# A two-layer attention and state-space backbone on one core: half of the chunk input matrices made one stage earlier, one state copy on another engine

## The chip, the core and the metric

The kernel runs on one core of a Trainium2 chip. Its time is the device time of one execution in microseconds (us); lower is better. The engines are TensorE (PE in the profile; PEld is its weight load), VectorE (DVE), ScalarE (ACT), GpSimd (POOL) and SyncE (SP), which here only issues DMAs.

## What is computed

The reference is a backbone of two layers over 2048 latent tokens and 256 context tokens of width 1024, all in float32. Layer 0 is windowed attention with sinks; layer 1 is a bidirectional diagonal state-space layer (S5), and only layer 1 is touched here. Cut to that:

```python
u, z = split(h @ w_in, 2);  uc = hc @ w_in[:, :1024]     # 64 groups of 16 channels
for dirn in range(2):
    a_bar = exp(lam * dt);  b_bar = ((a_bar - 1) / lam)[..., None] * b_mat     # complex, 64 states per group
    bu = einsum('gph,blgh->blgp', b_bar, u)              # 'bu_c' the same for the context
    xs = diag_scan(a_bar, bu with the context's end state added)               # second direction on flipped rows
    y += einsum('ghp,blgp->blgh', c_mat, xs).real
out = ((glu(gelu(y) @ w_glu)) * silu(z)) @ w_out
```

The kernel cuts the 2304 tokens into 144 chunks of 16. What one chunk adds to the 64 complex states of a group is a product of the chunk's 16 x 16 inputs with a matrix E[t, h] = a_bar^(15 - t) * b_bar[h], a power of a_bar times a column of b_bar: these are the chunk input matrices, 2 (real, imaginary) x 64 groups of [128 x 256], where the 128 partitions are 2 directions x 64 states.

## The kernel before

Layer 1 goes through these stages.

**u projection** (`phase3`, lines 1236 to 1306). For u = 0 to 7, each a pair of row tiles, `prep(u + 1)` loads rows of x by DMA (SP queue, L1255), norms them, transposes them on TensorE, and splits them into a high and a low part (`split`, L106 to L111); `mm(u, j, n)` then multiplies with weights already in SBUF, three matmuls per product (L116 to L118), and ScalarE copies the result into `uy` (L1287). Beside it, `ssm_bc` (from L384) makes the tables of c and b and stores them in the DRAM tensor `tabd`; it is a generator that is stepped once per u for u = 1 to 5. `tabd[sl]` holds, for 8 groups, the powers (rows 0, 1) and b_bar (rows 2, 3).

**Chunk states** (`phase4`, lines 1309 to 1399). For sl = 0 to 7 (8 groups each) it loads `tab` from `tabd` (L1340) and the context's u (L1342), and copies the latter into place on VectorE (`uc`, L1350). For each half `hf` (4 groups) it makes the real and imaginary chunk matrices `er`, `ei`: two products and a sum each, with one product of each pair on GpSimd (`em`, L1365 and L1368), the other and the sum on VectorE (L1366, L1367, L1369, L1370). `er` and `ei` have two buffers each, one per half. For each group TensorE transposes E (four transposes into `ep`, L1382; ScalarE copies them to `esb`, L1384), transposes u (`up`, L1389 and L1390; three of four are copied back by VectorE, L1394, one by ScalarE, L1392), and one group behind multiplies both into `st` (L1329, `chunk_states`; two PSUM buffers). Three ScalarE copies take `st` to `sall`: the forward states (L1331), and the backward states in reversed order in two parts (L1332, L1333). In `sall` the group is the innermost index, so that a copy writes single floats at a stride.

**Scan and z projection** (`scan` from L1405, `zproj` from L1427). The scan over the 143 chunks is a chain of products and sums on VectorE alone (L1420, L1425). Meanwhile TensorE does the z projection (tiles `zps`), whose weights and rows are loaded over SP (L1445, L1457, tile `zraw`) and split. Its SBUF tiles lie over those of the stage before: a load starts when the tile below it has had its last reader. The first product of the scan is pinned, by `keep`, behind the VectorE instructions written before it, which are the splits of the first weights and of the first two row pieces.

**Outputs** (`phase5`, `phase6`, `phase7`) follow; none of their lines is edited.

The source is not the order of issue: a planner simulates the program and gives each engine's queue its order, which is then fixed. Each queue runs in order, and an instruction that waits holds up all behind it.

Of the kernel before, what the change touches and what calls it, by code (L numbers as in the profile page):

```python
# [6 lines left out]
F32 = mybir.dt.float32  # L7
# [3 lines left out]
AF = mybir.ActivationFunctionType  # L11
OP = mybir.AluOpType
# [60 lines left out]
P3O = 'P0 C01 C11 P1 M00 M10 M01 M11'  # L73
LO = 'x21 yt0 ogh1 gate1 zt0 zt1 vt1 x20 ogh2 ogh3 ogl2 ogl3 ogh0 ogl0 ogl1 gate0 vt0'
LO4 = 'tab4_0 tab4_1 em_0 uc4_1 uc4_0 esb_0 esb_1 esb_2 esb_3 ucr4_0 er_0 ei_0 em_1 er_1 ei_1'
UCA = 'vvvvvvvv'
HP = 0
ZC = 5
# [7 lines left out]
class Net:  # L86
# [1149 lines left out]
    def phase3(self, uy):  # L1236
        nc, a = self.nc, self.a
        with ExitStack() as es:
            es.callback(self.kpool.__exit__, None, None, None)
            es.callback(self.esm3.close)  # L1240
            es.callback(self.es3.close)
            ex, wq, sq = self.ex3, self.wu, self.sq3
            x0 = self.xp3.tile([128, 2, D], F32, name="xt3")
            for j in range(2):
                nc.sync.dma_start(x0[:, j], self.xrows(j))
            xh = ex.enter_context(self.pool("p3xh", 1, side="right"))
            sm = es.enter_context(self.pool("p3s", 2))
            ps = es.enter_context(self.pool("p3ps", 2, PSUM))
            H = {-1: self.hc}

            def prep(u):
                if u:
                    xs = self.kp.tile([128, 2, D], F32, name=("qta", "qtb")[u % 2])
                    for j in range(2):
                        nc.sync.dma_start(xs[:, j], self.xrows(2 * u + j))  # L1255
                else:
                    xs = x0
                ss = sq.tile([128, 2], F32, name="ss3")
                for j in range(2):
                    junk = sq.tile([128, D], BF16, name="junk3", bufs=1)  # L1260
                    nc.scalar.activation(junk, xs[:, j], AF.Square, accum_out=ss[:, j:j + 1])
                r = self.rstd(sq, ss, 2)
                for j in range(2):
                    (nc.vector if u == 0 and j == 0 else nc.gpsimd).tensor_scalar(xs[:, j], xs[:, j], r[:, j:j + 1], 1.0, op0=OP.mult,
                                                                                  op1=OP.mult)
                hi = sm.tile([128, KT, 256], F32R, name="hi3")
                lo = sm.tile([128, KT, 256], F32R, name="lo3")
                for k in range(0, KT, 2):
                    self.prep3(k, lambda j, c: xs[:, j, c:c + 128], ps.tile([128, 2, 256], F32, name="tp3"), hi, lo, 0,
                               self.h1d[u][:, k:k + 2],  # L1270
                               xh.tile([128, 2, 256], F32, name=f"hf{k}") if u == 0 and k < 4 else None)
                H[u] = (hi, lo)

            def mm(u, j, n):
                hi, lo = H[u]
                c = slice(j * 128, (j + 1) * 128)
                p = self.mmp.tile([128, 512], F32, name="mm3")
                for q in range(2):
                    w = wq[n * 2 + q]
                    self.mm3(p[:, q * 256:(q + 1) * 256], lambda k: hi[:, k, c], lambda k: lo[:, k, c],  # L1280
                             lambda k: w[0][:, k], lambda k: w[1][:, k], KT)
                if u < 0:
                    self.ctx_out(j, n, p)
                    return
                for q in range(4):
                    o = uy[n * 4 + q][:, :, (15 - 2 * u - j) * 16:(16 - 2 * u - j) * 16]
                    nc.scalar.activation(o, p[:, q * 128:(q + 1) * 128].rearrange("p (g h) -> p g h", h=16), AF.Copy)  # L1287

            for tok in P3O.split():
                if tok[0] == "P":  # L1290
                    prep(int(tok[1]))
                else:
                    mm(0 if tok[0] == "M" else -1, int(tok[1]), int(tok[2]))
            for u in range(1, 8):
                if u + 1 < 8:
                    prep(u + 1)
                for j in range(2):
                    for n in range(2):
                        mm(u, j, n)
                if u == 1:  # L1300
                    ex.close()
                    bp = es.enter_context(self.pool("p3b", 1, side="right"))
                    bps = es.enter_context(self.pool("p3bps", 1, PSUM))
                    bc = self.ssm_bc(bp, bps)
                if 1 <= u <= 5:
                    next(bc)


    def phase4(self, uy, sall):
        nc, a = self.nc, self.a  # L1310
        with ExitStack() as es:
            pool4 = es.enter_context(self.pool("p4", 1))
            size4 = {"tab4": 512, "ucr4": 2048, "uc4": 2048, "esb": 512}
            for nm in LO4.split():
                pool4.tile([128, size4.get(nm.split("_")[0], 1024)], F32, name=nm)
            turn = {}

            def T4(name, shape, n):
                i = turn[name] = turn.get(name, -1) + 1
                return pool4.tile(shape, F32, name=f"{name}_{i % n}")  # L1320

            ps = es.enter_context(self.pool("p4ps", 2, PSUM))
            pend = []

            def chunk_states(esb, u, g):
                st = ps.tile([128, 2, 144], F32, name="st", bufs=PB[2])
                for ri in range(2):
                    for b in range(2):
                        nc.tensor.matmul(st[:, ri], esb[:, ri, b], u[:, b * 144:(b + 1) * 144], start=b == 0, stop=b == 1)  # L1329
                sv = sall.rearrange("p j r g -> p r j g")  # L1330
                nc.scalar.activation(sv[0:64, :, :, g], st[0:64], AF.Copy)  # L1331
                nc.scalar.activation(self.rev(sall, 64, 128, 15, 16, g), st[64:128, :, 0:16], AF.Copy)  # L1332
                nc.scalar.activation(self.rev(sall, 64, 128, 143, 128, g), st[64:128, :, 16:144], AF.Copy)  # L1333

            for sl in range(8):
                hp4 = ExitStack()
                if sl < HP:
                    hp4.enter_context(self.tc.manual_schedule(engines={nc.vector.engine}))
                tab = T4("tab4", [128, 4, 8, 16], 2)
                nc.sync.dma_start(tab, self.tabd[sl, :, 0:4].rearrange("p j (g h) -> p j g h", g=8))  # L1340
                ucr = T4("ucr4", [16, 16, 128], 1)
                nc.sync.dma_start(ucr, self.ucd[:, sl * 128:(sl + 1) * 128].rearrange("(c t) n -> c t n", t=16))  # L1342
                uc = T4("uc4", [16, 8, 256], 2)
# [2 lines left out]
                cv = ucr.rearrange("c t (g h) -> c t g h", h=16)  # L1346
                if UCA[sl] == "a":
                    nc.scalar.activation(uv, cv, AF.Copy)
                else:
                    (nc.vector if UCA[sl] == "v" else nc.gpsimd).tensor_copy(uv, cv)  # L1350
                E = []
                for hf in range(2):
                    gs = slice(hf * 4, hf * 4 + 4)

                    def pw(j):
                        return tab[:, j, gs, :, None].to_broadcast([128, 4, 16, 16])

                    def bb(j):
                        return tab[:, 2 + j, gs, None, :].to_broadcast([128, 4, 16, 16])

                    er = T4("er", [128, 4, 16, 16], 2)
                    ei = T4("ei", [128, 4, 16, 16], 2)
                    m = T4("em", [128, 4, 16, 16], 2)
                    m2 = T4("em", [128, 4, 16, 16], 2)
                    nc.gpsimd.tensor_tensor(m, pw(1), bb(1), op=OP.mult)  # L1365
                    nc.vector.tensor_mul(er, pw(0), bb(0))  # L1366
                    nc.vector.tensor_sub(er, er, m)  # L1367
                    nc.gpsimd.tensor_tensor(m2, pw(1), bb(0), op=OP.mult)  # L1368
                    nc.vector.tensor_mul(ei, pw(0), bb(1))  # L1369
                    nc.vector.tensor_add(ei, ei, m2)  # L1370
                    E.append((er, ei))
                hp4.close()
                for hf in range(2):
                    er, ei = E[hf]
                    for gg in range(4):
                        g = sl * 8 + hf * 4 + gg
                        gl = hf * 4 + gg
                        ep = ps.tile([128, 2, 2, 128], F32, name="ep", bufs=PB[0])
# [7 lines left out]
                        u = uy[sl][:, gl]  # L1386
# [543 lines left out]
    def run(self, dbg=None):  # L1930
        nc, tc, a = self.nc, self.tc, self.a
        with ExitStack() as es:
            dr = es.enter_context(tc.tile_pool(name="dram", bufs=1, space=DRAM))
# [2 lines left out]
            self.vd = dr.tile([NTILE, 128, 4, 128], F32, name="vd")  # L1936
            self.zd = dr.tile([NTILE, 128, 8, 128], F32, name="zd")
            self.x1d = dr.tile([NTILE, 128, D], F32, name="x1d")
            self.modd = [dr.tile([2, 3 * D], F32, name=f"mod{i}") for i in range(2)]
            self.tabd = dr.tile([8, 128, 9, 128], F32, name="tabd")  # L1940
            self.a16d = dr.tile([128, 2, 64], F32, name="a16d")
# [16 lines left out]
            with self.pool("sall", side="right") as sp:  # L1958
                sall = sp.tile([128, 144, 2, 64], F32, name="sall")
# [63 lines left out]
```

## Time and profile before

| | us |
|---|---|
| median of 3 runs (2672.64 to 2676.73) | 2673.79 |
| the profiled execution | 2675.37 |
| its span, first to last instruction | 2673.5 |
| TensorE busy | 2540.4 (95%) |
| VectorE busy | 1624.3 (61%) |
| ScalarE busy | 1190.1 (45%) |
| GpSimd busy | 933.2 (35%) |

Busy shares are averages over unlike stages, and a TensorE matmul's recorded time includes its pipeline, so that back-to-back matmuls overlap in the record. The stages have to be read one by one. All starts below are us from the start of the span.

### The profile page before, as it was taken

Reading aid. Unit: us, or ns where it says so; the run is one execution under the profiler, and the core shown is the slowest. Engines: PE = TensorE matmul, PEld = TensorE weight load, DVE = VectorE, ACT = ScalarE, POOL = GpSimd, SP = SyncE. Lnnn points to the kernel's source line nnn. Section 1 sums busy time; section 2 is a strip of 40 time slices with the busy share of each in tenths; the row PEclk is TensorE's granted clock in tenths of the full one; section 3 lists DMA queues with packets and bytes.
Section 4 is the critical chain, followed back from the end, with each engine's and each line's share of the span. In section 5 each row is a group of like instructions: output and inputs, shape, how many; then the busy total and the mean of one; then the engine's idle time right before and its main releaser. Section 6 shows DMA issues by size and latency. Waiting matters only on the chain. (4 is left out here: it accounts for less than half of the span.)

```text
span 2673.5 us, 43894 instructions
## 1 busy us (share of the span) xinstructions
PE 2540.4 (95%) x15973; PEld 2273.4 (85%) x15973; DVE 1624.3 (61%) x3816; ACT 1190.1 (45%) x2711; POOL 933.2 (35%) x778
## 2 busy tenths in 40 slices
PE   7999999998999999999899999899489899999998
PEld 5999989987988999998899988899467688888887
DVE  4772377537888888888531288799976431002454
ACT  3201210137777777777443178633189820001221
POOL 0321331213554455555241163355255222221221
PEclk9999999999999999999999989999789999999999
DMA  8464446477453434343363100344133332223542
GB/s 285 166 180 140 141 153 191 140 206 183 109 127 96 105 99 118 84 109 106 110 168 99 32 25 13 118 143 156 49 91 94 94 86 63 81 61 122 170 143 85
DMA packets 374330, 317.22 MB, mean 119 GB/s; under 512 B 64210, under 2 KB 327394, under 8 KB 374114
## 3 DMA queue, kind: packets, MB, share of 16 engines
q1 hardware_dynamic: 264722, 235.64, 31.8%
q10 hardware_dynamic: 109392, 78.76, 9.2%
q8 instruction: 127, 2.08, 0.3%
q14 instruction: 89, 0.73, 0.1%
HBM read 225.63 MB, written 88.70 MB: 118 GB/s over the span
## 5 line engine op out<-in xcount | busy, mean ns | idle before, releaser
L116 PE MATMUL mm<-hhl,whi 128*128 128x384 f32 x848 | 286.9, 341 | 3.6 <-DVE whi L108 2.7
L934 POOL TENSOR_SCALAR P<-P,ri 128x640 f32<-128x640 f32 (+2 forms) x272 | 208.7, 780 | 228.4 <-DVE ri L932 187.4
L117 PE MATMUL mm<-hhl,whi 128*128 128x384 f32 x848 | 286.8, 338 | 0.0
L118 PE MATMUL mm<-hhl,wlo 128*128 128x384 f32 x848 | 285.2, 337 | 0.6 <-DVE wlo L111 0.6
L953 DVE TENSOR_TENSOR pl<-pt,ph 128x512 fp32r<-128x512 f32 (+1 forms) x384 | 233.2, 607 | 32.6 <-ACT ph L952 30.0
L912 DVE CUSTOM_DVE_ANT_0 P<-S,mask,sink 128x640 f32<-128x640 f32 (+1 forms) x240 | 209.2, 872 | 55.9 <-PE S L903 50.6
L952 ACT ACTIVATE ph<-pt 128x512 fp32r<-128x512 f32 (+1 forms) x384 | 202.9, 529 | 73.2 <-PE pt L948 70.5
L948 PE MATMUL pt<-ident,P 128*128 128x128 f32 x1312 | 212.6, 274 | 13.0 <-DVE pl L953 5.2
L913 ACT ACTIVATE P<-P,nm 128x640 f32<-128x640 f32 (+1 forms) x256 | 208.1, 813 | 23.7 <-DVE nm L912 7.7
L948 PEld LDWEIGHTS pt<-ident,P 128*128 128x128 f32 x1312 | 156.6, 140 | 31.3 <-POOL P L934 10.8
L111 POOL TENSOR_TENSOR wlo<-wraw,whi 128x512 fp32r<-128x512 f32 x60 | 86.6, 1472 | 259.0 <-DVE whi L108 252.7
L116 PEld LDWEIGHTS mm<-hhl,whi 128*128 128x128 f32 x848 | 159.5, 189 | 14.3 <-issue 9.9
L117 PEld LDWEIGHTS mm<-hhl,whi 128*128 128x128 f32 x848 | 160.2, 189 | 6.5 <-issue 6.1
L118 PEld LDWEIGHTS mm<-hhl,wlo 128*128 128x128 f32 x848 | 160.0, 189 | 1.3 <-DVE wlo L111 0.9
L116 PE MATMUL zps<-zh,wzh 128*128 128x256 f32 x512 | 146.0, 287 | 5.1 <-ACT zo L1496 4.3
L117 PE MATMUL zps<-zh,wzh 128*128 128x256 f32 x512 | 146.2, 287 | 2.4 <-POOL zh L111 2.4
L1852 DVE TENSOR_TENSOR gy<-gps,gs 128x512 f32<-128x512 f32 x32 | 22.1, 691 | 207.4 <-POOL gs L1850 207.4
L118 PE MATMUL zps<-zh,wzl 128*128 128x256 f32 x512 | 145.9, 286 | 0.0
L1425 DVE TENSOR_TENSOR sall<-sall 128x64 f32<-128x64 f32 x560 | 141.6, 309 | 0.1
L1849 ACT ACTIVATE gs<-gps 128x512 f32<-128x512 f32 x32 | 19.1, 597 | 258.6 <-PE gps L118 258.6
L108 DVE CAST whi<-wraw 128x512 fp32r<-128x512 f32 (+1 forms) x80 | 53.5, 719 | 106.7 <-PE mm L117 86.7
L111 POOL TENSOR_TENSOR zh<-zraw,zh 128x512 fp32r<-128x512 f32 x61 | 81.6, 1344 | 101.6 <-ACT zh L106 78.3
(591 smaller groups left out, 7735.3 us busy)
## 6 DMA issues: line engine op xcount, KB each, us to landing
qta<-qd SPq DMA_DIRECT2D x144, 128.0 KB
qtb<-qd SPq DMA_DIRECT2D x144, 128.0 KB
wraw<-in_w_ada_dram SPq DMA_DIRECT2D x16, 1024.0 KB
zraw<-h1d SPq DMA_DIRECT2D x64, 256.0 KB
wraw<-in_attn_w_in_dram SPq DMA_DIRECT2D x12, 1024.0 KB
mq<-qqd SPq DMA_DIRECT2D x64, 192.0 KB
qd<-oh ACTq DMA_DIRECT2D x48, 192.0 KB
qd<-ol ACTq DMA_DIRECT2D x48, 192.0 KB
```

The lines of the kernel that those rows point to most:

```text
L108: nc.vector.tensor_copy(hi, src)
L111: (nc.gpsimd if lo_eng == "g" else nc.vector).tensor_tensor(lo, src, hi.bitcast(F32), op=OP.subtract)
L116: nc.tensor.matmul(ps, whi(k), mhi(k), start=first and k == 0, stop=False)
L117: nc.tensor.matmul(ps, whi(k), mlo(k), start=False, stop=False)
L118: nc.tensor.matmul(ps, wlo(k), mhi(k), start=False, stop=last and k == nk - 1)
L912: nc.vector.tensor_tensor_reduce(o, sc, mk, -0.125, nsink[:, h:h + 1], OP.add, OP.min, nm)
L913: nc.scalar.activation(p, p, AF.Exp, bias=nm, scale=-1.0, accum_out=SM[i][:, e:e + 1])
L934: (nc.vector if e >= CTXV else nc.gpsimd).tensor_scalar(P[i][e], P[i][e], ri[:, e:e + 1], 1.0, op0=OP.mult, op1=OP.mult)
L948: ins = nc.tensor.transpose(t[:, c - c0], P[i][e][:, k * 128:(k + 1) * 128], self.ident)
L952: nc.scalar.activation(ph[:, c0:c1], t, AF.Copy)
L953: nc.vector.tensor_tensor(pl[:, c0:c1], t, ph[:, c0:c1].bitcast(F32), op=OP.subtract)
L1425: nc.vector.tensor_add(y[:, :, hs[h]], t[:, h, i], y[:, :, hs[h]])
```

## The change

Three edits. (1) For sl = 0, 2, 4, 6 the chunk matrices are made in the u projection by a new generator, `chunk_in`: 16 pieces of 2 groups, at u = 3 to 6, each with six VectorE instructions (one product goes to PSUM, none to GpSimd) and two DMAs of 256 KB to a new DRAM tensor `ed`; `phase4` then loads `er` and `ei` from `ed` in four DMAs of 512 KB per sl, and leaves out `tab` and the making for these. (2) The steps of `ssm_bc` come earlier: two at u = 1, two at u = 2, one at u = 3; then its SBUF pool is closed and a pool for the pieces opened. (3) The larger part of the backward states' copy (L1333) goes from ScalarE to VectorE.

```diff
+PRE = (0, 2, 4, 6)
...
-                if 1 <= u <= 5:
+                for _ in range((0, 2, 2, 1, 0, 0, 0, 0)[u]):
                     next(bc)
+                if u == 3:
+                    eb.close()
+                    ep = es.enter_context(self.pool("p3e", 2, side="right"))
+                    eg = self.chunk_in(ep, bps)
+                if u >= 3:
+                    for _ in range(4):
+                        next(eg, None)
+            for _ in eg:
+                pass
+
+    def chunk_in(self, pool, ps):
+        nc = self.nc
+        for sl in PRE:
+            tab = pool.tile([128, 4, 8, 16], F32, name="tab3", bufs=1)
+            nc.sync.dma_start(tab, self.tabd[sl, :, 0:4].rearrange("p j (g h) -> p j g h", g=8))
+            for hq in range(4):
+                gs = slice(hq * 2, hq * 2 + 2)
...
+                for ri, op in enumerate((OP.subtract, OP.add)):
+                    e = pool.tile([128, 2, 16, 16], F32, name="e3" + "ri"[ri])
+                    m = ps.tile([128, 512], F32, name="ctp2", bufs=1).rearrange("p (g t h) -> p g t h", g=2, t=16)
+                    nc.vector.tensor_mul(e, pw(0), bb(ri))
+                    nc.vector.tensor_mul(m, pw(1), bb(1 - ri))
+                    nc.vector.tensor_tensor(e, e, m, op=op)
+                    nc.sync.dma_start(self.ed[sl, ri, :, hq * 512:(hq + 1) * 512], e.rearrange("p g t h -> p (g t h)"))
+                yield
...
-                nc.scalar.activation(self.rev(sall, 64, 128, 143, 128, g), st[64:128, :, 16:144], AF.Copy)
+                nc.vector.tensor_copy(self.rev(sall, 64, 128, 143, 128, g), st[64:128, :, 16:144])
...
-                tab = T4("tab4", [128, 4, 8, 16], 2)
-                nc.sync.dma_start(tab, self.tabd[sl, :, 0:4].rearrange("p j (g h) -> p j g h", g=8))
+                if sl not in PRE:
+                    tab = T4("tab4", [128, 4, 8, 16], 2)
+                    nc.sync.dma_start(tab, self.tabd[sl, :, 0:4].rearrange("p j (g h) -> p j g h", g=8))
...
+                    if sl in PRE:
+                        for ri, e in enumerate((er, ei)):
+                            nc.sync.dma_start(e.rearrange("p g t h -> p (g t h)"),
+                                              self.ed[sl, ri, :, hf * 1024:(hf + 1) * 1024])
+                        E.append((er, ei))
+                        continue
```

## Rows read from the trace of the kernel before

**Rows 1.** Busy time by stretch: start:end, length, engine busy (instructions), clock, DMA share, GB/s.
```profile
1420.00:1530.00 110.00, 110.00 (x940) 110.00 (x940) 13.99 (x33) 30.94 (x109) 17.09 (x12) 1.00 0.18 59
1530.60:1697.90 167.30, 159.24 (x1041) 133.95 (x1040) 134.06 (x131) 128.47 (x276) 73.80 (x32) 0.94 0.10 28
1697.90:1928.40 230.50, 191.62 (x1550) 188.06 (x1548) 228.92 (x878) 72.52 (x159) 100.91 (x80) 0.92 0.41 125
```

**Rows 2.** Timeline of TensorE after the z projection: start, us, instruction, idle before.
```profile
1929.76 3.78 PE L1669 MATMUL yp<-uy,xT 128*128 128x256 f32 x8 [32.68 <-ACT xT L1664]
```

**Rows 3.** Timeline of TensorE, two matmul groups of the steady part of `phase4`.
```profile
1653.00 1.25 PE L1329 MATMUL st<-uy,esb 128*128 128x144 f32 x8
...
1655.31 1.25 PE L1329 MATMUL st<-uy,esb 128*128 128x144 f32 x8
```

**Rows 4.** Timelines where `phase4` begins: a wait of TensorE, then one of VectorE.
```profile
1534.39 0.23 PE L1390 MATMUL up<-ident,uc 16*128 16x16 f32 x1 [3.31 <-DVE uc L1350]
...
1527.96 1.23 DVE L1369 TENSOR_TENSOR ei<-tab 128x1024 f32<-128x1024 f32 x1 [14.65 <-PE mm L118]
```

**Rows 5.** Timeline of TensorE around a stall in the middle of `phase4`.
```profile
1594.55 0.33 PE L1389 MATMUL up<-ident,uy 128*128 128x128 f32 x1 [0.77 <-DVE uy L1394]
...
1595.39 1.52 PE L1329 MATMUL st<-uy,esb 128*128 128x144 f32 x8
...
1602.86 1.32 PE L1329 MATMUL st<-uy,esb 128*128 128x144 f32 x8
```

**Rows 6.** Waits of TensorE in `phase4`: us in total, times, longest.
```profile
PE st L1329 <- ACT sall L1333: 3.4, 11, 0.6
```

**Rows 7.** Timelines where `phase4` hands over: TensorE, SP queue, VectorE, TensorE.
```profile
1687.53 0.38 PE L1382 MATMUL ep<-ident,ei 128*128 128x128 f32 x2
...
1688.37 5.67 SPq L1457 DMA_DIRECT2D zraw<-h1d  x4
...
1695.48 1.38 DVE L1420 TENSOR_TENSOR kps<-sall,bco 128x128 f32<-128x128 f32 x1
...
1696.12 0.38 PE L116 MATMUL zps<-zh,wzh 128*128 128x256 f32 x1
```

**Rows 8.** Groups of VectorE in `phase4`: busy us, mean ns, idle before and releaser.
```profile
L1370 DVE TENSOR_TENSOR ei<-ei,em 128x1024 f32<-128x1024 f32 x16 | 33.2, 2077 | 1.5 <-POOL em L1368 1.5
L1366 DVE TENSOR_TENSOR er<-tab 128x1024 f32<-128x1024 f32 x15 | 24.1, 1608 | 9.5 <-PE ep L1382 9.5
L1369 DVE TENSOR_TENSOR ei<-tab 128x1024 f32<-128x1024 f32 x15 | 23.4, 1560 | 0.0
L1367 DVE TENSOR_TENSOR er<-er,em 128x1024 f32<-128x1024 f32 x16 | 21.1, 1317 | 1.5 <-POOL em L1365 1.5
L1394 DVE COPY uy<-up 128x288 f32<-128x288 f32 x48 | 21.0, 446 | 7.3 <-PE up L1390 7.2
L1350 DVE COPY uc<-ucr 16x2048 f32<-16x2048 f32 x8 | 13.3, 1665 | 0.4 <-DMA ucr<-ucd 0.4
```

**Rows 9.** Group of ScalarE in `phase4`: the copy that moves.
```profile
L1333 ACT ACTIVATE sall<-st 64x256 f32<-64x256 f32 x64 | 38.5, 602 | 0.0
```

**Rows 10.** One VectorE line before: a copy read at a stride, duration ns min/median/max.
```profile
L365 DVE COPY pwg<-pr x1: 1082/1082/1082, 537.9 to 537.9; 64x1024 f32<-64x1024 f32 x1
```

**Rows 11.** VectorE lines of 512 elements: sum in SBUF; product into PSUM (ns min/median/max).
```profile
L425 DVE TENSOR_TENSOR bx<-bx,by x4: 676/690/1604, 1353.5 to 1378.7; 128x512 f32<-128x512 f32 x4
...
L1536 DVE TENSOR_TENSOR ytp<-tab x4: 685/894/1111, 1928.4 to 1933.2; 128x512 f32<-128x512 f32 x4
```

**Rows 12.** Timelines: two loads of 512 KB issued, and the reader of the second.
```profile
1439.68 0.81 SPq L1255 DMA_DIRECT2D qtb<-x1d  x2
...
1446.16 1.06 ACT L1261 ACTIVATE junk<-qtb 128x1024 bf16<-128x1024 f32 x1 [1.19 <-DMA qtb<-x1d]
```

**Rows 13.** Timelines: last split of `prep(7)` on GpSimd, first matmul of u = 7.
```profile
1490.98 1.29 POOL L111 TENSOR_TENSOR lo<-kctx,hi 128x512 fp32r<-128x512 f32 x1 [2.40 <-DVE hi L108]
...
1507.90 0.28 PE L116 MATMUL mm<-kall,hi 128*128 128x256 f32 x1
```

More of the change, by code (lines that the diff above doesn't have):

```diff
@@ L1301, in phase3, with pw, bb @@
                     ex.close()
-                    bp = es.enter_context(self.pool("p3b", 1, side="right"))
+                    eb = ExitStack()
+                    bp = eb.enter_context(self.pool("p3b", 1, side="right"))
                     bps = es.enter_context(self.pool("p3bps", 1, PSUM))
                     bc = self.ssm_bc(bp, bps)
-                if 1 <= u <= 5:
+                for _ in range((0, 2, 2, 1, 0, 0, 0, 0)[u]):
                     next(bc)
+                if u == 3:
[14 more added lines that the diff above has]
+                gs = slice(hq * 2, hq * 2 + 2)
+                def pw(j):
+                    return tab[:, j, gs, :, None].to_broadcast([128, 2, 16, 16])
+                def bb(j):
+                    return tab[:, 2 + j, gs, None, :].to_broadcast([128, 2, 16, 16])
+                for ri, op in enumerate((OP.subtract, OP.add)):
[6 more added lines that the diff above has]
+                yield
     def phase4(self, uy, sall):
@@ L1938, in run @@
             self.x1d = dr.tile([NTILE, 128, D], F32, name="x1d")
+            self.ed = dr.tile([8, 2, 128, 2048], F32, name="ed")
             self.modd = [dr.tile([2, 3 * D], F32, name=f"mod{i}") for i in range(2)]
```

## The prediction

> **What bounds the kernel now.** I first read the busy times of three stretches around the edits [rows 1]. In the u projection (1420 to 1530) TensorE is busy in all 110 us, at the full clock; VectorE has 14.0 of 110. In `phase4` (1530.6 to 1697.9) the granted clock is 0.94 and VectorE has 134 of 167. In the scan (1697.9 to 1928.4) VectorE has 228.9 of 230.5: it alone sets the end, and TensorE, done early, stands idle for 32.7 us before the outputs [rows 2]. So the u projection can take VectorE work, and what counts at the other side is not when the z projection starts but when the scan starts.
>
> What does `phase4` cost at best? In its steady part TensorE goes from one group's `st` to the next in 2.31 us (1655.31 - 1653.00) [rows 3]; 64 groups make 147.8. The stage took 165.5, from its first transposes at 1530.6, where I set the edge of the stretch [rows 1], to the first `zps` matmul at 1696.1 [rows 7]. The 17.7 between them lie in three places. At the start TensorE waits 3.31 us for VectorE's `uc`, which stood behind chunk products [rows 4]. [...] At the end it waits 3.4 us for `st` buffers that ScalarE has not copied [rows 6]. The remainder, 10.7, I put down to the start: the 3.31 and the slow clock behind it, with about 2 of scatter.
>
> How does this stage hand over? The scan's first product is pinned behind splits of rows whose loads need the tiles of E. The last transposes of E end at 1687.9 (1687.53 + 0.38); the loads go out at 1688.4, and the scan starts at 1695.5, 7.6 after the last transposes [rows 7]. The last `st` ends only at 1696, since transposes ran ahead of the ScalarE-bound `st`.
>
> **The change, part by part.**
> *Making in `phase4`.* The four making lines hold 101.8 us of VectorE [rows 8]; half of it goes, 51, and half of their partner products on GpSimd.
>
> *The moved copy.* ScalarE loses 64 x 0.602 = 38.5 us [rows 9], from 128 to 90 of 167: the 3.4 at the end goes. VectorE gains 64 copies. No row shows one that writes single floats at a stride. From the PSUM copy of 288 columns, 446 ns [rows 8], 256 columns cost at least 0.40 each, 25.6 in all; as on ScalarE, 0.60, they would be 38.5. [...] With the copies of `up` (21.0) and `uc` (13.3) VectorE then has 51 + 25.6 + 34.3 = 111 us in some 155, or 124 at the dear end.
>
> But it is uneven. A half's E can be made only while the other half is consumed, 4 x 2.31 = 9.2 us, and takes 101.8 / 16 = 6.4 on average. With three copies of `up` (1.3), four new copies (1.6) and half a `uc` (0.8) that window needs 10.1 of 9.2, twice in a row for each of sl = 1, 3, 5, 7; in the windows of the loaded halves it needs 3.7. TensorE can fill by transposing u ahead, as it does now. I count one stall as now, 3.6, between none and the eight windows' 8 x 3.6 = 29.
>
> *Loads of E.* Two 512 KB loads issued together had the second one in use 6.5 us after issue (1446.16 - 1439.68) [rows 12], within the 9.2: no wait in the middle. At the start, the first half's real part can come early, and so can `uc` with no chunk product ahead of it; the imaginary part lies over what matmuls of the projection read until 1528.0 [rows 4], so even two thirds of that 6.5 reach to 1532, and u's transposes fill part of that. I allow 1.5 for the start, beside the 2 of scatter, in place of 10.7; nothing and the old 10.7 are the ends.
>
> *Pieces in the u projection.* 16 x 6 instructions of 512 elements: 0.69 each from the SBUF sum, 0.89 for the two into PSUM [rows 11], so 4.5 a piece, 73 us, beside 14 of 110. The four `tab3` loads have one buffer and hold VectorE for some 4 each: 103 of 110 at worst. Hidden, then; the cover is that `prep(7)`'s last split ends at 1492.3 and its first matmul comes at 1507.9, 15.6 later [rows 13]. Without it TensorE would wait for splits at full price. On SP, 32 stores and 4 loads at up to 0.5 us are 18 us of queue; each store waits for VectorE, and loads of x behind it wait too, but the last of these went out at 1439.7, long ahead of need. The 16 loads in `phase4` are 8 us of queue in a stage where SP is nearly empty.
>
> *`ssm_bc` earlier.* The same transposes, loads and stores, up to two u sooner; TensorE would wait only if a transpose stands ahead of its load's landing, 0 to 4 us. I take 0, since matmuls of u stand ready to go first.
>
> **The sum.** 147.8 + 1.5 + 2 + 3.6 = 154.9 for `phase4`, so it ends at 1685.5, 10.6 earlier. But the hand-over takes part of this back. With ScalarE no bound, the source's order leaves behind the last transposes of E that group's u (0.8) and two `st` (2.2): they end at 1682.5, only 5.4 earlier than 1687.9. The loads, splits and the pinned product keep their 7.6, so the scan starts 5.4 earlier; add 0.4 for less waiting beside its first steps, and 5.8 passes through to the end, because TensorE has 32.7 to spare there. 2675.4 - 5.8 = 2669.6 for the profiled execution, which stands 1.6 over the median: **2668.0**. A measurement of this kernel can tell about 0.2%, 5.3 us; the forecast lies on the edge of that.
>
> **The rivals.**
> *Nothing stalls (0.17).* VectorE, with 111 of 155, keeps up and the start is covered: 5.1 more (3.6 + 1.5) than above, a gain of 10.9, 2663. For: two idle engines and u's transposes to fill with. Against: the two full windows in each odd sl.
>
> *Given back at the hand-over (0.20).* Two more stalls of 3.6 as in the middle now, or a start like the old one: 2675. The change then does all it says and the scan starts where it did. For: the old stage had one such stall with VectorE at 80%. Against: half the making is gone.
>
> *VectorE's queue holds up `st` (0.16), slower.* The place is the moved copy behind a chunk sum. [...] 3.6 each; from three stalls (10.8 against 5.8 + 3.6) the change loses, and at five of the eight windows it is 14.4 more than one: 2682. A dear copy, at 0.60 or more, would bring this about.
>
> *The edit doesn't hide (0.02).* Lateness of over 15.6 us on VectorE in the u projection stops TensorE before u = 7; 2685.
>
> **How the numbers follow.** The forecast's own case has 0.45 and spans 2664 to 2672, two thirds of it on the faster side of 2668.4: 0.30 faster, 0.15 same. With 0.17 faster from the first rival, 0.18 same and 0.02 slower from the second, 0.16 and 0.02 slower from the last two: 0.47, 0.33, 0.20. The range leaves out half of the slower cases and the best of the first: 2660 to 2679.
>
> **What would show it.** Right: no wait on `uc` and full clock at the start of `phase4`; no TensorE wait on ScalarE at its end; `zraw` loads some 5 us earlier, the scan's first product about 7 us behind them; TensorE still full in the u projection; the moved copy near 0.40. Wrong: TensorE waiting for L1364's copies or for loads of E with the clock down, a scan that starts as late as before, or a gap in the u projection.

## The result, and the profile after

The changed kernel takes 2691.22 us (median of 4 runs, 2688.31 to 2693.69) where the kernel before takes 2673.22 beside it (2670.63 to 2676.73): a ratio of 1.0062, 95% interval 1.0044 to 1.0079. It is slower, and above the forecast's range. The profiled execution took 2692.82, its span is 2691.0.

I read the stretches first; the columns are those of [rows 1]. The lines are the u projection, `phase4` from the first transposes of u to the start of the last transpose of E, from there to the scan's first product, and the scan.

```profile
1423.00:1533.00 110.00, 110.00 (x938) 110.00 (x937) 78.10 (x127) 30.23 (x107) 13.84 (x10) 1.00 0.40 142
1533.70:1698.10 164.40, 149.88 (x977) 122.13 (x977) 114.82 (x144) 91.83 (x196) 34.06 (x16) 0.96 0.20 60
1698.10:1713.20 15.10, 9.72 (x58) 7.84 (x56) 8.41 (x16) 7.55 (x17) 0.34 (x1) 0.86 0.29 92
1713.20:1945.00 231.80, 195.14 (x1555) 192.53 (x1555) 229.69 (x879) 72.25 (x158) 102.29 (x81) 0.90 0.42 126
```

In the u projection VectorE went from 14 to 78 of 110 us, and TensorE is still full at the full clock: the making hides. In `phase4` the loads on VectorE (115) and ScalarE (92) lie where the forecast had them (111 to 124, and 90), and yet the stage is no shorter. The 17.5 us between the spans (2691.0 - 2673.5) lie as follows. The first transposes of u come 3.1 later (1533.7 for 1530.6), which no edit explains: the projection's results leave for `uy` over 188.5 us in both, and in the twelve kernels below this start lies anywhere from 1527.7 to 1534.8. From there to the last transpose of E it is 7.4 longer (164.4 for 157.0), from this to the scan's first product 7.2 longer (15.1 for 7.9), and behind that 0.2 shorter. The kernel before has its two marks here, each line with its first and last start:

```profile
L1389 PE MATMUL up<-ident,uy x128: 272/328/474, 1530.6 to 1671.7; 128*128 128x128 f32 x128
L1382 PE MATMUL ep<-ident,ei x128: 272/273/474, 1539.0 to 1687.6; 128*128 128x128 f32 x128
```

**The first 7.4.** The waits of TensorE from 1529 to 1715 (us in total, times, longest), where `st` waited for ScalarE alone in [rows 6]:

```profile
PE st L1363 <- DVE sall L1367: 7.5, 14, 1.4
...
PE ep L1423 <- ACT esb L1425: 5.0, 14, 0.8
...
PE up L1430 <- DVE uy L1435: 1.5, 1, 1.5
```

How most of them come about shows in one half of sl = 5, in the timelines of VectorE, ScalarE and TensorE:

```profile
1646.08 0.59 DVE L1367 COPY sall<-st 64x256 f32<-64x256 f32 x1
1646.70 2.43 DVE L1411 TENSOR_TENSOR ei<-ei,em 128x1024 f32<-128x1024 f32 x1
1649.16 1.04 DVE L1367 COPY sall<-st 64x256 f32<-64x256 f32 x2
```

```profile
1646.93 0.22 ACT L1366 ACTIVATE sall<-st 64x32 f32<-64x32 f32 x1
...
1648.01 0.68 ACT L1365 ACTIVATE sall<-st 64x288 f32<-64x288 f32 x1 [0.23 <-PE st L1363]
1648.70 0.22 ACT L1366 ACTIVATE sall<-st 64x32 f32<-64x32 f32 x1
1648.95 0.60 ACT L1425 ACTIVATE esb<-ep 128x512 f32<-128x512 f32 x1
1651.10 0.66 ACT L1365 ACTIVATE sall<-st 64x288 f32<-64x288 f32 x1 [1.56 <-PE st L1363]
1651.78 0.22 ACT L1366 ACTIVATE sall<-st 64x32 f32<-64x32 f32 x1
1652.03 0.60 ACT L1425 ACTIVATE esb<-ep 128x512 f32<-128x512 f32 x1
```

```profile
1649.82 1.25 PE L1363 MATMUL st<-uy,esb 128*128 128x144 f32 x8 [1.33 <-DVE sall L1367]
...
1652.68 0.44 PE L1423 MATMUL ep<-ident,er 128*128 128x128 f32 x2 [0.19 <-ACT esb L1425]
...
1654.10 0.44 PE L1423 MATMUL ep<-ident,er 128*128 128x128 f32 x2 [0.77 <-ACT esb L1425]
```

One group's ScalarE copies end at 1647.15. Its copy on VectorE could follow, but stands behind the chunk sum L1411, which runs from 1646.70 to 1649.13; then two copies go in a row. The first ends at 1649.76, its `st` buffer is free, and TensorE, idle for 1.33, starts at 1649.82. So the next `st` is late; ScalarE, whose queue has the copy of that `st` at its head, waits 1.56 for it, and the copy of `esb` behind it (1652.03) comes late too; then TensorE waits for `esb`. ScalarE's forward copy waits 63.1 us for TensorE over the stage, where it waited 27.0 before. TensorE has nothing to put into the gaps: its last transposes of u start at 1639.7, before at 1672.0. Of the 14 waits for the copy, nine, 6.5 of the 7.5 us, come behind a copy that stood ready for 2.0 to 5.6 us while VectorE worked on products, sums or `uc`. The other five come behind the last transposes, where nothing stands ahead of the copy: it starts 0.03 after ScalarE's, and TensorE waits 0.2 each.

A part of the loss lies at the start already. The stretches of the changed kernel to 1570 and from 1639.5, and the start in e1 (below), which differs by this copy alone:

```profile
1533.70:1570.00 36.30, 32.95 (x178) 25.10 (x177) 29.81 (x30) 13.61 (x31) 14.78 (x6) 0.81 0.23 69
1639.50:1706.30 66.80, 54.71 (x403) 48.34 (x402) 43.53 (x52) 48.62 (x102) 11.57 (x6) 1.00 0.15 48
1534.80:1570.00 35.20, 31.62 (x217) 25.78 (x216) 24.64 (x24) 23.50 (x52) 18.84 (x6) 1.00 0.37 111
```

While sl = 1 is made, two of the copies stand 4.2 and 5.6 us ready, and TensorE waits five times from 1548 to 1555, 2.5 us in all: for the two `st`, for E, and 1.5 for a copy of `up` behind `uc`. Then its granted clock falls, to 0.50 from 1556 to 1569 (the eight matmuls of an `st` take 2.29 instead of 1.15), so that it does 178 instructions here where e1 does 217. At the 6.4 per us of the stretch behind (448 in 69.5) this is about 6 us, an estimate. E1 waits about as long there and its clock stays at 1.00, so which of the waits took the clock down is not shown. After 1639.5 the clock is 1.00, and what is lost there is lost by waiting.

**The other 7.2** are the hand-over, the counterpart of [rows 7], in the timelines of TensorE, the SP queue and VectorE:

```profile
1697.99 0.38 PE L1423 MATMUL ep<-ident,ei 128*128 128x128 f32 x2
```

```profile
1698.83 0.98 SPq L1498 DMA_DIRECT2D zraw<-h1d  x2
```

```profile
1707.47 0.59 DVE L1367 COPY sall<-st 64x256 f32<-64x256 f32 x1 [0.83 <-ACT sall L1366]
1708.09 0.43 DVE L109 CAST wzh<-zraw 128x512 fp32r<-128x512 f32 x1
...
1713.24 1.37 DVE L1461 TENSOR_TENSOR kps<-sall,bco 128x128 f32<-128x128 f32 x1
```

The loads go out 0.5 after the last transposes, as before. But VectorE's queue now has the last copies of the states ahead of the casts of what they bring; the casts wait until 1708.09, and the splits with the scan behind them follow 5.2 later. Before, VectorE did those casts at 1690.8 and 1692.7, beside ScalarE's last copies.

### The profile page after: what moved, and what is told of

It reads as the page before. It is cut to its first block, busy times and chain, and to the rows that moved or that the text cites. A ratio compares the mean times of both kernels' runs of the same rounds, so it can differ in the third digit from the quotient of the medians.

```text
span 2691.0 us, 44023 instructions
## 1 busy us (share of the span) xinstructions
PE 2546.0 (95%) x15973; PEld 2275.4 (85%) x15973; DVE 1676.9 (62%) x3944; ACT 1160.0 (43%) x2647; POOL 892.8 (33%) x762
```

## The experiments

The kernels of one group ran beside the kernel before on one chip: the first four (before 2675.09), the next four (2674.49), the next two (2673.75), the last two (2673.93). Three starts are read from each trace: the first transpose of u, the last transpose of E, and the scan's first product. "Stage" is from the first to the second, "hand-over" from the second to the third; from there to the end it is 973 to 981 us in all.

| kernel | start | stage | hand-over | median | ratio, interval |
|---|---|---|---|---|---|
| before | 1530.6 | 157.0 | 7.9 | 2673.22 | |
| changed | 1533.7 | 164.4 | 15.1 | 2691.22 | 1.0062, 1.0044 to 1.0079 |
| e1_copy_back | 1534.8 | 150.0 | 7.3 | 2670.48 | 0.9988, 0.9977 to 0.9999 |
| e2_copy_only | 1534.5 | 175.5 | 15.2 | 2701.31 | 1.0104, 1.0086 to 1.0121 |
| e3_both_parts | 1529.1 | 161.7 | 14.9 | 2684.90 | 1.0040, 1.0025 to 1.0054 |
| e4_mixed | 1532.3 | 162.9 | 7.3 | 2680.96 | 1.0024, 1.0013 to 1.0035 |
| e5_in_a_row | 1534.6 | 161.6 | 14.6 | 2688.58 | 1.0046, 1.0031 to 1.0061 |
| e6_copy_in_tail | 1527.7 | 153.2 | 7.1 | 2670.32 | 0.9980, 0.9968 to 0.9991 |
| e7_first_only | 1531.0 | 148.8 | 7.9 | 2664.69 | 0.9959, 0.9944 to 0.9974 |
| e8_last_eight_back | 1532.9 | 165.1 | 7.6 | 2683.30 | 1.0034, 1.0024 to 1.0043 |
| e9_uc_on_scalar | 1533.5 | 153.3 | 7.2 | 2673.93 | 0.9999, 0.9986 to 1.0013 |
| e10_up_on_vector | 1530.6 | 153.7 | 7.6 | 2671.17 | 0.9994, 0.9980 to 1.0008 |
| e11_not_first | 1534.2 | 154.0 | 7.3 | 2672.96 | 1.0001, 0.9990 to 1.0012 |
| e12_first_only_again | 1531.9 | 148.7 | 7.6 | 2666.96 | 0.9979, 0.9967 to 0.9990 |

**Which of the two edits: e1 and e2.** The changed kernel with the copy back, and the kernel before with the copy alone moved:

```diff
-                nc.vector.tensor_copy(self.rev(sall, 64, 128, 143, 128, g), st[64:128, :, 16:144])
+                nc.scalar.activation(self.rev(sall, 64, 128, 143, 128, g), st[64:128, :, 16:144], AF.Copy)
```

> The changed kernel with the backward states' copy back on ScalarE; the matrices of half the sl are still made in the u projection. Theory A (the moved copy does the harm: it stands in VectorE's order behind sums of 1.2 to 2.8 us, holds st, and at the end holds the splits before the scan): the 14.5 us lost from the first transposes to the scan's first product come back and the gain forecast for the making appears: 2662 to 2670, TensorE waiting for ScalarE at most, the scan's first product within 8 us of the last transposes of E. Theory B (the harm is the uneven supply of E, loaded halves early and made halves late, with u's transposes used up by 1640): 2683 or more, with the same TensorE idle from 1640 on.

> The kernel before with nothing changed but the backward states' copy on VectorE. Theory A: VectorE had 134 of 167 us there and gets 64 x 0.60 = 38 more, so it becomes the bound: 2690 to 2710, TensorE waiting for the copy in phase4. Theory B: the copy takes 38 us from ScalarE and does no harm by itself: 2668 to 2676.

The copy alone costs what is lost, and more: e2 is 28 us slower than the kernel before (0.0104 x 2675), the stage 18.5 longer and the hand-over 7.3. With the copy back the making ahead is a small gain, 3 us by the ratio, whose interval ends just short of 1; the time, 2670.48, lies just past theory A's range. Its stage is 14.4 shorter than the changed kernel's, its hand-over 7.8. The waits of TensorE in e1 and e2, from 1529 to 1715:

```profile
PE st L1363 <- ACT sall L1367: 4.5, 16, 0.7
...
PE up L1430 <- DVE uy L1435: 2.1, 2, 1.5
```

```profile
PE st L1329 <- DVE sall L1333: 11.7, 15, 2.0
...
PE ep L1382 <- ACT esb L1384: 6.4, 13, 1.2
```

E2's waits are the changed kernel's two, larger, since there all eight sl are made on VectorE beside the copies. In e1 ScalarE's pace at the end is what is left, and two waits for copies of `up`.

**What orders the copies: e3.** The small part of the backward states goes to VectorE too, so that ScalarE has the forward states alone.

```diff
-                nc.scalar.activation(self.rev(sall, 64, 128, 15, 16, g), st[64:128, :, 0:16], AF.Copy)
+                nc.vector.tensor_copy(self.rev(sall, 64, 128, 15, 16, g), st[64:128, :, 0:16])
```

> The changed kernel with the small part of the backward states (16 of 144 columns) on VectorE as well, so that ScalarE writes the forward states alone. In the changed kernel each moved copy starts 0.03 us after ScalarE's small copy. If that is an order by the memory that both write, this copy now starts with ScalarE's forward copy, 0.9 us earlier, and st comes free earlier: 2682 to 2690. If it is an order by the PSUM tile that both read, VectorE's first copy waits for ScalarE's forward copy and the time stays or grows: 2690 to 2698.

The time is 2684.9, some 6 less than the changed kernel's by the ratios, and the stage 2.7 shorter. That is the time expected of an order by `sall`, but the wait is the one expected of an order by `st`; why the time fell all the same is not shown. VectorE's longest wait for ScalarE in `phase4`:

```profile
DVE sall L1366 <- ACT sall L1365: 20.6, 27, 1.4
```

VectorE's copies of partitions 64 to 127 wait for ScalarE's copy of partitions 0 to 63. They write different partitions, and in the timeline of the changed kernel ScalarE copies a later group (1648.01) ahead of VectorE's copy of an earlier one (1649.16): so the order seems to be kept over the one `st` tile that both read, and not over `sall`. Whether the two could read it side by side is not shown; no run here tried it.

**Where the copy stands: e4.** On VectorE only in the 28 groups of those halves in which VectorE was meant to make nothing, and never in the last eight.

```diff
+                if g < 56 and g // 4 % 4 in (0, 3):
+                    nc.vector.tensor_copy(self.rev(sall, 64, 128, 143, 128, g), st[64:128, :, 16:144])
+                else:
+                    nc.scalar.activation(self.rev(sall, 64, 128, 143, 128, g), st[64:128, :, 16:144], AF.Copy)
```

> The changed kernel with the copy on VectorE only in the halves during which VectorE makes no E (the first half of even sl, the second of odd sl, and none of sl 7), 28 of 64 copies, else on ScalarE. Theory A, in its form that the place behind the making does the harm: as good as with all copies on ScalarE or up to 4 us better, 2660 to 2668, with no wait of TensorE for VectorE's copies over 0.6. If the copy harms wherever it stands (0.60 each on VectorE, one engine waiting for the other): 2672 to 2685.

The hand-over is 7.3 again, but the stage 12.9 longer than in e1 with 28 copies of 64, and the time lies in the range of the theory that the copy harms wherever it stands. TensorE still waits 3.1 for VectorE's copies and 3.5 for `esb`. The edit didn't keep the copies clear of the chunk sums, though: in VectorE's timeline one stands at 1591.27 and the next at 1594.85, with a sum of 2.42 between them, and each of TensorE's five waits for such a copy follows one behind a product or a sum. At the start the clock falls here too: the eight matmuls of an `st` take 1.25 at 1549.27, 2.29 at 1559.33 and 1.15 at 1567.97. So this doesn't tell the two theories apart. What it shows is that 28 copies leave nearly all of the stage's loss (12.9 of 14.4), and that the hand-over is as before without copies in the last eight groups.

**The price: e5.** The copy writes its floats in a row, and so not where the scan reads them.

```diff
-                nc.vector.tensor_copy(self.rev(sall, 64, 128, 143, 128, g), st[64:128, :, 16:144])
+                s = sall[64:128]
+                o = bass.AP(tensor=s.tensor, offset=s.offset + 16 * 128 + g * 256, ap=[list(s.ap[0]), [128, 2], [1, 128]])
+                nc.vector.tensor_copy(o, st[64:128, :, 16:144])
```

> The changed kernel with one difference: the moved copy writes its 256 floats in a row instead of at a stride, so the backward states land at other places of sall and the result is not the reference's; all instructions, waits and partners are the same. Theory A, the stride of the writes makes the price: the copy falls from 0.60 us to about 0.40 (446 ns for the 288 columns of the copy of up), 64 x 0.20 = 13 us less on VectorE; the two late copies per half then take 0.6 instead of 1.04 us, and of the 14.6 us that the stretch from the first transposes of u to the scan lost, some 4 to 8 come back, 2683 to 2687. Theory B, the price is not the stride but the reading of PSUM or of half the partitions: the copy stays at 0.60 and the time at 2691. Theory C, the price is the stride but the harm is only the order (st copies one behind the other and behind chunk sums): the copy falls to 0.40 and the time stays within 3 us of 2691.

The copy of the changed kernel and of e5, one line each with its duration (ns, min/median/max):

```profile
L1367 DVE COPY sall<-st x64: 576/599/619, 1547.7 to 1707.5; 64x256 f32<-64x256 f32 x64
```

```profile
L1369 DVE COPY sall<-st x64: 420/427/429, 1548.2 to 1705.2; 64x256 f32<-64x256 f32 x64
```

The stride makes 0.17 of the 0.60. But 64 x 0.17 = 11 us less on VectorE give back 2.6 us of time by the medians, 4 by the ratios to the kernels before beside them, whose intervals overlap, with 2.8 in the stage. That is nearest to theory C: most of the harm is not what the copy costs.

**The hand-over by itself: e8.** The last eight groups' copies go back to ScalarE, the other 56 stay on VectorE.

```diff
+                if g < 56:
+                    nc.vector.tensor_copy(self.rev(sall, 64, 128, 143, 128, g), st[64:128, :, 16:144])
+                else:
+                    nc.scalar.activation(self.rev(sall, 64, 128, 143, 128, g), st[64:128, :, 16:144], AF.Copy)
```

> The changed kernel with the copy of the last 8 groups of 64 back on ScalarE, of the other 56 on VectorE. Theory A, 7.1 of the 14.6 us lost before the scan come from the casts for the z projection that stand behind VectorE's last copies: from the last transposes of E to the scan's first product it is 7.3 again instead of 14.7, and the time 2683 to 2685. Theory B, the scan's late start is only the late last st and ScalarE's copies set it as well: the last transposes come at the same time or later (8 groups at 1.88), the scan starts some 3 us earlier at most and the time is 2688 to 2691.

Theory A, in both numbers. VectorE at the hand-over of e8, where the last transposes of E start at 1698.0:

```profile
1701.05 0.43 DVE L109 CAST wzh<-zraw 128x512 fp32r<-128x512 f32 x1 [4.72 <-DMA zraw<-in_ssm_w_in_dram]
...
1705.58 1.37 DVE L1464 TENSOR_TENSOR kps<-sall,bco 128x128 f32<-128x128 f32 x1
```

The first cast now waits for its load and not for copies, and the scan starts 7.6 behind the transposes instead of 15.1. The last `st` starts as late as in the changed kernel (1706.4 for 1706.2): the scan's first product doesn't wait for it.

**The copy only where VectorE is free: e6.** On VectorE in groups 44 to 55.

```diff
+                if 44 <= g < 56:
+                    nc.vector.tensor_copy(self.rev(sall, 64, 128, 143, 128, g), st[64:128, :, 16:144])
```

> The changed kernel with the copy on VectorE only for groups 44 to 55 of 64, on ScalarE for all others. With the whole copy on ScalarE the last 19 groups went at ScalarE's pace of 1.88 us each, with it on VectorE at 1.43, and VectorE has its last chunk products behind it there. Theory A, the copy harms only where VectorE's queue holds chunk products or the splits for the scan: here it holds neither, so 12 x 0.45 = 5.4 us less from the first transposes of u to the scan than with the copy back on ScalarE (157.3), some 152, and 2665. Theory B, the copy harms wherever it stands, because it waits for ScalarE's copies of the same st: the stretch is 157 to 160 and the time 2670 to 2674.

Start to scan took 160.3, theory B's number, and the time is level with e1. But the premise didn't hold: in the trace a half of sl = 7 is made from 1656.45 to 1663.03, between the first of these copies, and TensorE waits 2.6 for those behind products and sums. For the four copies after the last sum, from 1672.36 on, it waits nowhere. It stays open whether a copy with no chunk sum near it would gain.

**What else VectorE might take: e10.** E1 with the sixteen copies of `up` that ScalarE did on VectorE.

```diff
-UPA = [1]
+UPA = []
```

> The changed kernel with the copy of the states back on ScalarE and, in its place, the sixteen copies of up that ScalarE did (every fourth group) on VectorE: 6.5 us leave ScalarE for 16 x 0.45 = 7.2 on VectorE, which was busy half of phase4 in that form. This copy is the only reader of its tile, so it stands behind no copy of another engine, and up has three buffers. Theory A, what VectorE may take is work that shares no tile with ScalarE's queue: ScalarE's tail, where the last 19 groups go at 1.88 us each, becomes up to 6.5 us shorter, and the stretch from the first transposes of u to the scan falls from 157.3 to 151 to 154, 2665 to 2668. Theory B, any copy on VectorE behind chunk products stops TensorE: TensorE waits for VectorE's copies of up at the making halves and the stretch is 158 or more, 2671 or more.

The stage is 3.7 longer than e1's and the time no different. VectorE, and TensorE behind it:

```profile
1552.27 2.94 DVE L1410 TENSOR_TENSOR ei<-tab 128x1024 f32<-128x1024 f32 x1
1555.13 1.17 DVE L1435 COPY uy<-up 128x288 f32<-128x288 f32 x3
```

```profile
1555.63 0.48 PE L1430 MATMUL up<-ident,uy 128*128 128x128 f32 x1 [2.40 <-DVE uy L1435]
```

Three copies stand behind two chunk products, TensorE waits 2.40, and the clock granted from 1545.4 to 1570 is 0.79, where e1 has 1.00. It is theory B, on a tile that VectorE shares with no other engine and that has three buffers.

**Which part of the making ahead pays: e7, e11 and e12.** With the copy on ScalarE, only sl = 0 is made ahead (e7, and e12 again), or only the three others (e11).

```diff
-PRE = (0, 2, 4, 6)
+PRE = (0,)
```

```diff
-PRE = (0, 2, 4, 6)
+PRE = (2, 4, 6)
```

> The changed kernel with the copy on ScalarE and with only sl = 0 made in the u projection and loaded; sl = 2, 4, 6 are made in phase4 as before. Theory A, the gain of making ahead is the start (no uc behind chunk products, full clock in the first 20 us): nearly all of the 7.6 us that the stretch from the first transposes of u to the scan gained stays, 157 to 159, 2670 to 2672. Theory B, the gain is spread over the stage, since VectorE's load of 80% costs stalls in the middle: the stretch is 161 to 164 and the time 2673 to 2676.

> The complement of the kernel that makes only sl = 0 ahead: copy on ScalarE, sl = 2, 4 and 6 made in the u projection and loaded, sl = 0 made in phase4 as before. Theory A, all of the gain is the start of phase4, where E of sl = 0 can be made only after the projection: here the start is as before (TensorE waits at the first uc or E with the clock down), the stretch from the first transposes of u to the scan is 162 to 166 and the time 2672 to 2677, no different from before. Theory B, making ahead is worth the same wherever it is: the stretch is 158 to 160, 2668 to 2671.

> The kernel that makes only sl = 0 ahead, with the copy on ScalarE, once more, beside its complement on one chip. Theory A: ratio to before 0.995 to 0.998 and at least 5 us less than the complement. Theory B: the complement, which makes three of the four ahead, is level with it or faster.

It is sl = 0. E7 and e12 are faster than the kernel before, e11 is level with it, and e12 is 6.0 less than e11 on the same chip. Stretches of 14.4 us at the start of the stage in the kernel before, in e11, with a wait of TensorE from its timeline, and in e12, columns as above (in e11 and e12 the stretch begins 1.2 and 0.9 ahead of the first transpose of u):

```profile
1530.60:1545.00 14.40, 11.09 (x47) 8.35 (x46) 12.51 (x11) 3.19 (x9) 9.12 (x4) 0.65 0.12 37
```

```profile
1533.00:1547.40 14.40, 11.09 (x53) 8.41 (x53) 12.69 (x11) 3.18 (x9) 9.84 (x4) 0.70 0.10 22
```

```profile
1538.05 0.23 PE L1431 MATMUL up<-ident,uc 16*128 16x16 f32 x1 [3.31 <-DVE uc L1385]
```

```profile
1531.00:1545.40 14.40, 14.40 (x103) 11.84 (x102) 7.89 (x10) 7.77 (x19) 6.72 (x2) 1.00 0.56 151
```

TensorE, with the first E loaded, does 103 instructions here instead of 47 or 53, at a clock of 1.00 where theirs is 0.65 and 0.70. This is the kernel to keep: 0.9979 (0.9967 to 0.9990) in e12, and 0.9959 in e7, on another chip.

**Is it the wait on `uc` alone: e9.** The kernel before with that first copy on ScalarE.

```diff
-UCA = 'vvvvvvvv'
+UCA = 'avvvvvvv'
```

> The kernel before with one edit: the first context copy uc (sl = 0) goes from VectorE, where it stands behind chunk products, to ScalarE, which is free 70% of the u projection; nothing is made ahead and the copies of the states stay on ScalarE. Theory A, the start of phase4 was lost to the wait on uc alone: TensorE has transposes of u to do from the first moment, its clock stays at 1.00, and the stretch from the first transposes of u to the scan falls from 164.9 to 157 to 159, 2667 to 2670. Theory B, it was lost to the first matrices E, whose imaginary part can only be made once the projection's matmuls are over (1527.96) and is ready at 1536.6: the transposes of u fill a part, then TensorE waits for er or ei instead, and the stretch is 161 to 165, 2671 to 2675.

The time is the kernel before's. But in ScalarE's order the copy came behind the last copies of the projection, at 1534.4, so that the wait was not removed:

```profile
1536.30 0.23 PE L1390 MATMUL up<-ident,uc 16*128 16x16 f32 x1 [2.30 <-ACT uc L1348]
```

This doesn't tell the wait on `uc` from that on E; the share of each stays open. It also shows how far one trace may be read: e9 and e11 have a stage 3 to 4 shorter than the kernel before's one profile, at the same median time.

## Why the prediction was wrong, point by point

**The start: right.** 10.7 were to become 3.5, 7.2 less. TensorE's longest wait for `uc` in the changed kernel is 0.39 (at 1545.4), and e7 and e12, which have this gain alone, have a stage 8.2 and 8.3 shorter than the one profile of the kernel before. Against e11, which lacks this gain alone, e12's stage is 5.3 shorter and its time 6.0 less, so its size is 5 to 8. The changed kernel lost it again by 1570: its 178 instructions in 36.3 us stand against 215 in 39.4 in the kernel before, whose clock there is 0.83.

**Pieces in the u projection: right.** The forecast had 73 us, hidden. The groups of VectorE there:

```profile
L1337 DVE TENSOR_TENSOR ctp<-tab 128x512 f32<-128x512 f32 x32 | 24.4, 763 | 0.3
L1336 DVE TENSOR_TENSOR e3i<-tab 128x512 f32<-128x512 f32 x16 | 12.4, 775 | 0.8 <-DMA ed<-e3i 0.5
L1336 DVE TENSOR_TENSOR e3r<-tab 128x512 f32<-128x512 f32 x16 | 11.8, 739 | 7.1 <-DMA tab<-tabd 6.6 <-DMA ed<-e3r 0.4
L1338 DVE TENSOR_TENSOR e3i<-e3i,ctp 128x512 f32<-128x512 f32 x16 | 11.0, 687 | 0.5
L1338 DVE TENSOR_TENSOR e3r<-e3r,ctp 128x512 f32<-128x512 f32 x16 | 10.9, 684 | 0.2
```

They sum to 70.5, the loads of `tab3` cost 6.6 in three waits, and TensorE is full throughout. The loads of E in `phase4` stop nothing, as forecast: no wait for one stands among those from 1529 to 1715.

**The moved copy at 0.40: wrong, but of little weight.** It takes 0.60, the dear end of the bounds. The strided read of [rows 10], 1.06 ns for each element, had made me take the cheap end; it was no guide to a strided write: e5, with only the stride gone, has 0.43, near the 0.40. By e5 the mis-sized price is worth 3 to 4 us of the time at most.

**"I count one stall as now, 3.6": the step that failed.** The moved copy cost the stage 14.4 us (e1), not 3.6. The 3.6 is worked out from [rows 5]: 7.47 us between the two `st` where two groups of [rows 3] make 4.62, and the wait of 0.77 ahead of them; the clock granted over the 7.47 was 0.56. I had summed a window's work, 10.1 us in 9.2, and let TensorE fill the excess with transposes of u. Two things were missing. The copy's place: `st` has two buffers, and a copy behind a sum of 2.4 us holds one of them, in each half of sl = 5 and 7; the queue of ScalarE passes the delay on to `esb`. In the making of sl = 1 the clock fell as well (0.50 from 1556 to 1569). And the fill runs out: u is used up at 1639.7, with a third of the stage to go. Busy shares (115 and 92 of 164) can't show this; the copy left ScalarE, which was busy 77% [rows 1] but had it at once behind the `st` it follows, for VectorE, where it stands behind whatever is there.

**"The loads, splits and the pinned product keep their 7.6": the second that failed.** They kept it only while VectorE was idle at the end of `phase4`, ScalarE being late. The moved copies are exactly the work that takes that idle time; 15.1 was measured, and e8 gives the 7.5 back by moving eight copies. I had listed the pinned splits and not asked what now stands ahead of them on their engine.

**ScalarE's wait at the end: gone, as forecast, and worth nothing**, since the copies on VectorE came in its place.

**The rivals.** The slower one was it: VectorE's queue holds up `st`, with a copy of 0.60. Its place is the one measured. Its price, 3.6 for each stall with the clock down as in [rows 5], is not: in the stage the clock fell at sl = 1 alone, and the late halves cost waiting at the full clock (1.00 from 1570 to 1706.3). So it is in part luck that its time of 2682 is short of 2691 by about the hand-over, which it didn't have. The other three don't fit: nothing was given back at the start, and the u projection hid its part. For the making ahead without the copy, the forecast's gain of 5.8 would have been about right (e1: 3 by the ratio, 7.6 from start to scan).

## What to carry to other kernels

A copy that frees a buffer of the busiest engine belongs on the engine whose queue is short at that moment, not on the one with the lower busy share: read what stands ahead of it in the queue, how long that is, and how many buffers wait. Before an idle stretch of an engine is filled, look for the work at its far end that relied on it, here the splits that the scan is pinned behind. And when work is moved ahead of a stage, try the first piece alone: here one sl of four gave all of the gain.

## What the runs showed of the hardware that I had not expected

A write of single floats at a stride costs VectorE: it takes 0.60 us for 256 floats at a stride and 0.43 in a row, with nothing else changed (e5). Two further comparisons show less. ScalarE in the changed kernel takes 0.66 for the 288 of the forward states at a stride (L1365, 64 partitions) and 0.41 for 288 in a row (L1433, another tile, 128 partitions). VectorE's strided read of [rows 10] has 1.06 ns for each element, less than the 1.67 of the copy from PSUM that writes in a row (427 / 256), but it is longer, reads SBUF, and no run has it without its stride.
